# Wider products for the low-rank columns and the values of a hybrid decoder layer, and a shorter split of its norm weight

## The chip, the cores and the metric

The kernel runs on one core of a Trainium2 chip. The metric is the device time of one execution in microseconds: 638.64 us in the median of three runs before the change, between 638.29 and 639.48. Beside the times there is a profile of one execution, taken by the hardware profiler.

## The reference

One decoder layer with two parallel branches over 512 tokens of width 1024, everything in float32. `@` is a matrix product.

```python
h = rms_norm(x, norm_g)
hq, hf, hi, hz, cq, ckv, kr, mz, glog = split(h @ w_in)   # 4 x 1024 | 384 | 256 | 64 | 1024 | 2048
# branch a: 8 heads of 128, gated linear recurrence in chunks of 32 tokens
f = lb + (1 - lb) * sigmoid(hf);  q = silu(hq);  k = 1 - f;  v = hi
S_t = diag(f_t) S_{t-1} + k_t v_t^T;   o_t = S_t^T q_t
y_a = rms_norm(o per head, hg_norm_g) * silu(hz)
# branch b: 8 heads of attention over low-rank keys, queries and values
q    = rms_norm(cq, q_a_g) @ w_uq       # per head 128 without and 64 with a rotary position
k, v = rms_norm(ckv, kv_a_g) @ w_ukv    # per head 128 + 128; one rotary key kr for all heads
y_b  = softmax(causal(q k^T * scale)) v * silu(mz)
m = sigmoid(g_a) * (y_a @ w_proj_a) + sigmoid(g_b) * (y_b @ w_proj_b)   # g = glog + b_gate
out = rms_norm(x + m @ w_out, final_norm_g)
```

## The kernel before

Every large matrix product is done three times. An operand is split into a rounded high part and the rest (`hi`, `lo`), and `mm3` (L87) adds hi x hi, hi x lo and lo x hi in PSUM: its three matmuls are L90, L91 and L92. `load_w` (L94) brings a piece of weights of up to 128x1024 by SyncE's queue into one of three raw buffers, ScalarE rounds it (L111), VectorE subtracts (L112); there are four buffers each for the high and the low parts. Three PSUM tiles of 128x512 (`mm_tile`) take the large products, five more (`ax_tile`) the small ones.

The work runs in this order:

1. The start (L195 to L328), whose order on TensorE, ScalarE and VectorE is written out by hand. The norm weight comes as one row on one partition (L196), is split there (L270, L271), laid on the first row of two cleared tiles of 128x1024, and spread over all partitions by four matmuls with a matrix of ones (L274). Idle matmuls (`idle_mm`) stand between. Each 128-token tile of x is scaled by its norm factor and the spread weight (L237, `scaled`), turned by transposes (L245), and split into `hT` (L247, L248). The first 256 low-rank columns are multiplied in between (`c_product`, L256), and two weight loads for the next 256 are issued at the last tile (L320).
2. The other low-rank columns (L364): 256 and then 192, by `proj_tok` (L133). There a 128x128 block of `hT` is the stationary operand and the weights move, so one product is as wide as the columns. Two token tiles share a PSUM tile. The columns are normed and turned into `cT` (L368 to L396).
3. The recurrence, two heads at a time (`hg_pair`, L531). A pair has four stages of large products: forget, values, query and gate. Forget, query and gate are made by `proj_ch` (L120): the weights are stationary, `hT` moves with 512 tokens, and a stage fills two PSUM tiles. The values are made by `proj_tok` with 256 columns, two heads, and copied out by ScalarE (L538). From the forget product, VectorE and GpSimd make the decayed keys (`hg_forget`, L423: tanh L427, scan L432, reciprocal L433, then L448 to L451), from the query product `hg_query` makes the decayed queries (L459 to L463). Some working tiles there have one buffer for both heads.  `hg_states`, `hg_scores` and `hg_out` do the small products.
4. The attention, one head at a time (L691 to L711): scores and softmax, the rotary queries on every second head, the gate, the next head's keys and queries, the values of two heads on every even head (`mla_values`, L588: two k-steps, 256 columns), the product with the values of the head before (`mla_out`, L657) and the transposes of the probabilities (L652).
5. The merge of the branches (L730 to L743), the output product (L768 to L783) and the last norm, a token tile at a time. ScalarE scales and sends the first 512 columns of a tile (L793, L794), VectorE and SyncE's queue the others (L795, L796).

Behind the start, a scheduler puts the instructions of all engines in order when the program is built, by the order of the program and the times it estimates; an instruction that isn't ready can be passed by a later one then, but not when the program runs.

Of the kernel before, what the change touches and what calls it, by code (L numbers as in the profile page):

```python
# [9 lines left out]
F32 = mybir.dt.float32  # L10
# [28 lines left out]
def hybrid_layer(ctx: ExitStack, tc: tile.TileContext, a):  # L39
# [93 lines left out]
    def proj_tok(mat, c0, w, lhs, halves=None):  # L133

        halves = halves or load_cols(mat, c0, w)
        ps = []
        for t2 in range(NT // 2):
            b = mm_tile()
            for t in range(2):
                tt = 2 * t2 + t  # L140
                for kk in range(KD):
                    mm3(b[:, t * 256 : t * 256 + w], lhs, halves[kk // 4],
                        (slice(None), kk, slice(tt * P, tt * P + P)), (slice(None), kk % 4),
                        kk == 0, kk == KD - 1)
            ps.append(b)
        return ps
# [26 lines left out]
    ones = st.tile([P, P], F32, "ones")  # L173
    ones_r = st.tile([P, P], F32R, "ones_r")
    warm = st.tile([P, 1], F32, "warm")
    ng_row = st.tile([1, D], F32, "ng_row")
    ng_z = st.tile([P, D], F32, "ng_z")
    ng_r = [st.tile([P, D], F32R, f"ng_r{i}") for i in range(2)]
# [17 lines left out]
    nc.scalar.dma_start(ng_row[:], a["norm_g"])  # L196
# [61 lines left out]

    FIN = 1
    with tc.manual_schedule(engines={mybir.EngineType.PE, mybir.EngineType.Activation, mybir.EngineType.DVE}):  # L260
        nc.vector.memset(zero[:], 0.0)
# [8 lines left out]
        nc.vector.tensor_copy(ng_r[0][0:1], ng_row[:])  # L270
        nc.vector.tensor_tensor(ng_r[1][0:1], ng_row[:], ng_r[0][0:1].bitcast(F32), op=ALU.subtract)  # L271
        for x in range(2):
            for n in range(2):
                nc.tensor.matmul(ng[n][:], ones_r[:], ng_r[x][:, half[n]], start=x == 0, stop=x == 1)  # L274
            idle_mm(3)
# [36 lines left out]
        for t in range(1, NT):  # L312
# [153 lines left out]
    def hg_states(h, k128, ft, v_sb):  # L466
# [7 lines left out]
        for i in range(NT - 1):  # L474
            sl = slice(i * P, i * P + P)
            nc.tensor.matmul(sps[:, sl], kt_[:, sl], v_sb[:, i, (h % 2) * P : (h % 2) * P + P], start=True, stop=True)  # L476
# [25 lines left out]
    def hg_out(h, asb, st_, q128, v_sb):  # L502

        ops = ax_tile()
        for i in range(NT):
            sl = slice(i * P, i * P + P)
            nc.tensor.matmul(ops[:, sl], asb[:, sl], v_sb[:, i, (h % 2) * P : (h % 2) * P + P], start=True, stop=i == 0)  # L507
# [22 lines left out]

    def hg_pair(pair, before_gate=None, before_out=None):  # L531
# [159 lines left out]
    for h in range(H):  # L691
# [9 lines left out]
        if h % 2 == 0:  # L701
            v = mla_values(h // 2)
# [137 lines left out]
```

## Time and profile before

| | |
|---|---|
| median of three runs | 638.64 us |
| the profiled execution's own time | 638.65 us |
| its span, from the first to the last instruction | 636.9 us |
| TensorE busy | 627.3 us, 3539 matmuls |
| VectorE, ScalarE, GpSimd busy | 353.9, 239.4, 115.4 us |
| mean granted TensorE clock | 0.997 |
| moved by the DMA engines | 59.80 MB |

The profile is a page and a set of views on the trace of one execution. Engines are PE (TensorE matmul), PEld (TensorE weight load, which overlaps PE), DVE (VectorE), ACT (ScalarE), POOL (GpSimd) and SP (SyncE); a name with a q is that engine's queue of DMAs. A row of the timeline has the start in us, the duration in us, engine, line, operation, the tile written and those read, shapes, and how many instructions of one kind follow each other; behind it, in brackets, the idle time of the engine before it and what ended it. A group of the page has a count, the total busy time, the mean of one in ns, and the idle time in front. Matmuls are pipelined, so that their durations overlap: how long a stage takes is seen from starts.

### The profile page before, as it was taken

How to read it: one execution, taken by the hardware profiler on the slowest of the kernel's cores; microseconds unless marked ns; L12 is line 12 of the kernel's file. 1: busy time of each engine (PE TensorE's matmuls, PEld its weight loads, DVE VectorE, ACT ScalarE, POOL GpSimd, SP SyncE). 2: the span in 40 equal slices, each digit the busy share in tenths (PEclk: the TensorE clock that was granted, in tenths of full speed). 3: DMA queues.
4: the chain of work that ended last, by engine and by line, in shares of the span. 5: the costliest groups of instructions: out<-in, count | busy, mean ns of one | idle time of the engine just before them, and what ended most of it. 6: DMA issues, size and time to landing. Idle time of an engine off the chain costs nothing.

```text
span 636.9 us, 9069 instructions
## 1 busy us (share of the span) xinstructions
PE 627.3 (99%) x3539; PEld 540.1 (85%) x3539; DVE 353.9 (56%) x550; ACT 239.4 (38%) x453; POOL 115.4 (18%) x213
## 2 busy tenths in 40 slices
PE   8999999999999999999999999999999999999995
PEld 5998988988898898888888988888888888888884
DVE  7716973785486387547485857845322342434244
ACT  5535333232322323345454555534222232323223
POOL 2105310320331132221223132000000010111011
PEclk9999999999999999999999999999999999999998
DMA  7443242233124013312324142133333323324403
GB/s 248 137 125 100 67 138 62 67 99 100 34 68 131 13 55 102 92 45 66 104 56 115 51 138 78 37 100 99 100 98 94 98 75 102 102 95 158 173 11 121
DMA packets 61945, 59.80 MB, mean 94 GB/s; under 512 B 5799, under 2 KB 57293, under 8 KB 61902
## 3 DMA queue, kind: packets, MB, share of 16 engines
q1 hardware_dynamic: 59628, 55.47, 29.3%
q10 hardware_dynamic: 2130, 3.22, 1.6%
q8 instruction: 28, 0.46, 0.3%
q0 software_dynamic: 144, 0.52, 0.3%
q14 instruction: 15, 0.12, 0.1%
HBM read 55.01 MB, written 2.10 MB: 90 GB/s over the span
## 4 chain that ended last, share of the span: by engine, by line
PE 97%; DVE 1%; ACT 0%; issue 0%; POOLq 0%; POOL 0%
PE mm_ps L90 26%; PE mm_ps L92 26%; PE mm_ps L91 26%; PE ax_ps L91 2%; PE ax_ps L90 2%; PE ax_ps L92 2%; PE ax_ps L631 2%; PE mm_ps L256 1%; PE ax_ps L652 1%; PE ax_ps L488 1%; PE ax_ps L507 1%; PE ax_ps L509 1%; PE ax_ps L476 1%; PE ax_ps L496 1%; PE ax_ps L493 1%; PE ax_ps L523 1%
## 5 line engine op out<-in xcount | busy, mean ns | idle before, releaser
L112 DVE TENSOR_TENSOR w_lo<-w_raw,w_hi 128x1024 fp32r<-128x1024 f32 (+3 forms) x92 | 109.0, 1186 | 114.5 <-ACT w_hi L111 110.0
L90 PE MATMUL mm_ps<-hT,w_hi 128*128 128x512 f32 x384 | 151.3, 394 | 0.0
L111 ACT CAST w_hi<-w_raw 128x1024 fp32r<-128x1024 f32 (+3 forms) x92 | 89.8, 977 | 163.0 <-PE mm_ps L91 110.6
L92 PE MATMUL mm_ps<-hT,w_lo 128*128 128x512 f32 x384 | 150.2, 392 | 0.0
L91 PE MATMUL mm_ps<-hT,w_hi 128*128 128x512 f32 x384 | 149.8, 390 | 0.0
L92 PEld LDWEIGHTS mm_ps<-hT,w_lo 128*128 128x128 f32 x384 | 72.1, 188 | 14.8
L91 PEld LDWEIGHTS mm_ps<-hT,w_hi 128*128 128x128 f32 x384 | 72.2, 188 | 14.3
L90 PEld LDWEIGHTS mm_ps<-hT,w_hi 128*128 128x128 f32 x384 | 72.2, 188 | 14.1
L92 PE MATMUL mm_ps<-w_hi,hT 128*128 128x256 f32 (+1 forms) x192 | 54.1, 282 | 0.0
L91 PE MATMUL mm_ps<-w_lo,hT 128*128 128x256 f32 (+1 forms) x192 | 54.0, 282 | 0.0
L90 PE MATMUL mm_ps<-w_hi,hT 128*128 128x256 f32 (+1 forms) x192 | 54.0, 282 | 0.0
L742 POOL TENSOR_TENSOR ma<-ma,z 128x512 f32<-128x512 f32 x8 | 11.8, 1478 | 161.3 <-DVE z L741 161.3
L639 POOL TENSOR_SCALAR p<-p,sm 128x128 f32<-128x128 f32 (+3 forms) x32 | 20.6, 647 | 105.1 <-DVE sm L638 53.5
L91 PEld LDWEIGHTS mm_ps<-w_lo,hT 128*128 128x128 f32 x192 | 36.5, 190 | 0.2
L90 PEld LDWEIGHTS mm_ps<-w_hi,hT 128*128 128x128 f32 x192 | 36.4, 190 | 0.2
L92 PEld LDWEIGHTS mm_ps<-w_hi,hT 128*128 128x128 f32 x192 | 36.5, 190 | 0.0
L433 DVE RECIPROCAL tf<-pr 128x512 f32<-128x512 f32 x8 | 26.8, 3349 | 0.2
L637 ACT ACTIVATE p<-ax_ps,sm 128x128 f32<-128x128 f32 (+3 forms) x32 | 16.8, 528 | 22.0 <-DVE sm L636 21.5
L90 PE MATMUL mm_ps<-ya,w_hi 128*128 128x512 f32 x64 | 25.0, 390 | 0.0
L91 PE MATMUL mm_ps<-ya,w_hi 128*128 128x512 f32 x64 | 24.9, 389 | 0.0
L92 PE MATMUL mm_ps<-ya,w_lo 128*128 128x512 f32 x64 | 24.9, 389 | 0.0
L92 PE MATMUL mm_ps<-yb,w_lo 128*128 128x512 f32 x64 | 24.9, 389 | 0.0
(224 smaller groups left out, 1142.7 us busy)
## 6 DMA issues: line engine op xcount, KB each, us to landing
w_raw<-w_in SPq DMA_DIRECT2D x60, 512.0 KB, 3.8
w_raw<-w_proj_a SPq DMA_DIRECT2D x8, 512.0 KB, 3.5
w_raw<-w_proj_b SPq DMA_DIRECT2D x8, 512.0 KB, 3.4
wo_raw<-w_out SPq DMA_DIRECT2D x8, 512.0 KB, 3.2
w_raw<-w_ukv SPq DMA_DIRECT2D x16, 128.0 KB, 2.5
xr<-x SPq DMA_DIRECT2D x4, 512.0 KB, 6.5
x<-x SPq DMA_DIRECT2D x3, 512.0 KB, 8.7
w_raw<-w_uq SPq DMA_DIRECT2D x8, 192.0 KB, 2.6
```

Source lines behind the costliest of these rows:

```text
L90: nc.tensor.matmul(ps, lh[lsl], rh[rsl], start=start, stop=False)
L91: nc.tensor.matmul(ps, lh[lsl], rl[rsl], start=False, stop=False)
L92: nc.tensor.matmul(ps, ll[lsl], rh[rsl], start=False, stop=stop)
L111: nc.scalar.copy(hi[:, :o], raw[:, :o])
L112: (lo_eng or nc.vector).tensor_tensor(lo[:, :o], raw[:, :o], hi[:, :o].bitcast(F32), op=ALU.subtract)
L256: nc.tensor.matmul(ps, hT[l][:, 4 * kh + k, t * P : t * P + P], c_hl[kh][r][:, k * 256 : k * 256 + 256], start=kh == 0 and kind == 0 and k ...
L433: nc.vector.reciprocal(rp[:], pr[:])
L476: nc.tensor.matmul(sps[:, sl], kt_[:, sl], v_sb[:, i, (h % 2) * P : (h % 2) * P + P], start=True, stop=True)
L631: nc.tensor.matmul(sps[:, :n], qh[:, bl], kpe[x][:, :n], start=False, stop=x == 1)
L637: nc.scalar.activation(p[:, :n], sps[:, :n], AF.Exp, scale=SCALE, bias=sm[:, 1:2], accum_out=sm[:, 2:3])
L639: nc.gpsimd.tensor_scalar(p[:, :n], p[:, :n], sm[:, 3:4], 0.5, op0=ALU.mult, op1=ALU.mult)
L742: nc.gpsimd.tensor_tensor(ma[:, j], ma[:, j], g[:], op=ALU.add)
```

## The change

Five things are edited.

- The norm weight is laid as two rows of 512, on partitions 0 and 32 of a tile of 64 partitions, by two loads into a tile that GpSimd has cleared. It is split 512 wide. A selecting matrix (`pick`) takes the place of the ones, the clearing and copying of the large tiles on VectorE goes, and fewer idle matmuls stand between the first and the second pair of products (1 in place of 3; 4 in place of 3 behind the second).
- The low-rank columns are 256 and 448, not 256, 256 and 192. The weights come in four loads of two k-steps x 448; two are issued at the last tile of the start, two behind it. Each token tile has a PSUM tile of its own.
- The values of the recurrence are made for four heads at once, on pairs 0 and 2 alone: 512 columns, weights in four loads of two k-steps x 512. Two token tiles are done at a time, k outside and the tiles inside, so that the first two token tiles use all four loads and the second two use them again. They are kept in four tiles of 128x512 with one buffer each.
- The values of the attention are made for four heads at once, at heads 0 and 4, one token tile per PSUM tile, and kept in one buffer. They now stand behind the product with the head before.
- In the last norm the two halves of a tile lie in one buffer, and ScalarE and VectorE share the last token tile as 384 and 640 columns.

```diff
-    def proj_tok(mat, c0, w, lhs, halves=None):
-        halves = halves or load_cols(mat, c0, w)
-        ps = []
+    def proj_tok(mat, c0, lhs, done):
+        v = mat[:, c0 : c0 + 512].rearrange("(k p) c -> p k c", p=P)
+        w = []
         for t2 in range(NT // 2):
-            b = mm_tile()
+            ps = [mm_tile() for _ in range(2)]
+            for k in range(KD):
+                if t2 == 0 and k % 2 == 0:
+                    w.append(load_w(v[:, k : k + 2, :]))
+                for t in range(2):
+                    tt = 2 * t2 + t
+                    mm3(ps[t][:], lhs, w[k // 2], (slice(None), k, slice(tt * P, tt * P + P)), (slice(None), k % 2),
+                        k == 0, k == KD - 1)
             for t in range(2):
-                tt = 2 * t2 + t
-                for kk in range(KD):
-                    mm3(b[:, t * 256 : t * 256 + w], lhs, halves[kk // 4],
-                        (slice(None), kk, slice(tt * P, tt * P + P)), (slice(None), kk % 4),
-                        kk == 0, kk == KD - 1)
-            ps.append(b)
-        return ps
+                done(2 * t2 + t, ps[t])
...
+    ng_row = st.tile([64, 512], F32, "ng_row")
+    ng_r = [st.tile([64, 512], F32R, f"ng_r{i}") for i in range(2)]
+    nc.gpsimd.memset(ng_row[:], 0.0)
+    nc.gpsimd.memset(pick[:], 0.0)
+    for n in range(2):
+        nc.gpsimd.memset(pick[32 * n : 32 * n + 1, n], 1.0)
...
-    nc.scalar.dma_start(ng_row[:], a["norm_g"])
+    for n in range(2):
+        nc.scalar.dma_start(ng_row[32 * n : 32 * n + 1, :], a["norm_g"][:, n * 512 : n * 512 + 512])
...
+    w_c1 = w_in[:, COL_C + 256 : COL_C + 704].rearrange("(k p) c -> p k c", p=P)
+    def load_c2(j):
+        return load_w(w_c1[:, 2 * j : 2 * j + 2, :])
...
-        nc.vector.memset(ones[:], 1.0)
-        nc.vector.tensor_copy(ones_r[:], ones[:])
-        nc.vector.memset(ng_z[:], 0.0)
-        for i in range(2):
-            nc.vector.tensor_copy(ng_r[i][:], ng_z[:])
+        nc.vector.tensor_copy(pick_r[:], pick[:])
...
-        nc.vector.tensor_copy(ng_r[0][0:1], ng_row[:])
-        nc.vector.tensor_tensor(ng_r[1][0:1], ng_row[:], ng_r[0][0:1].bitcast(F32), op=ALU.subtract)
+        nc.vector.tensor_copy(ng_r[0][:], ng_row[:])
+        nc.vector.tensor_tensor(ng_r[1][:], ng_row[:], ng_r[0][:].bitcast(F32), op=ALU.subtract)
         for x in range(2):
             for n in range(2):
-                nc.tensor.matmul(ng[n][:], ones_r[:], ng_r[x][:, half[n]], start=x == 0, stop=x == 1)
-            idle_mm(3)
+                nc.tensor.matmul(ng[n][:], pick_r[:, n], ng_r[x][:], start=x == 0, stop=x == 1)
+            idle_mm(1 + 3 * x)
...
-                c_second = load_cols(w_in, COL_C + 256)
+                c_second = [load_c2(j) for j in range(2)]
...
-    for c0, w in ((0, 256), (256, 256), (512, 192)):
-        for t2, ps in enumerate(proj_tok(w_in, COL_C + c0, w, hT, c_second if c0 == 256 else None) if c0 else c_ps):
-            nc.scalar.copy(c_sb[:, 2 * t2 : 2 * t2 + 2, c0 : c0 + w],
-                           ps[:].rearrange("p (t c) -> p t c", t=2)[:, :, :w])
+    for t2, ps in enumerate(c_ps):
+        nc.scalar.copy(c_sb[:, 2 * t2 : 2 * t2 + 2, 0:256], ps[:].rearrange("p (t c) -> p t c", t=2))
+    c_second += [load_c2(j) for j in range(2, 4)]
+    for t in range(NT):
+        ps = mm_tile()
+        for k in range(KD):
+            mm3(ps[:, 0:448], hT, c_second[k // 2], (slice(None), k, slice(t * P, t * P + P)), (slice(None), k % 2),
+                k == 0, k == KD - 1)
+        nc.scalar.copy(c_sb[:, t, 256:704], ps[:, 0:448])
...
-        vps = proj_tok(w_in, COL_I + cc, 256, hT)
-        v_sb = hw.tile([P, NT, 256], F32, "v", 2)
-        for t2 in range(2):
-            nc.scalar.copy(v_sb[:, 2 * t2 : 2 * t2 + 2].rearrange("p t c -> p (t c)"), vps[t2][:])
+        if pair % 2 == 0:
+            for t in range(NT):
+                v_sb[t] = hw.tile([P, 512], F32, f"v{t}")
+            proj_tok(w_in, COL_I + cc, hT, lambda t, ps: nc.scalar.copy(v_sb[t][:], ps[:]))
...
-    def mla_values(pair):
-        wv = load_w(w_ukv[:, :, 2 * pair : 2 * pair + 2, 128:256])
-        v = [mw.tile([P, NT, 256], F32R, f"v{i}", 2) for i in range(2)]
-        for t2 in range(2):
+    def mla_values(h0):
+        wv = load_w(w_ukv[:, :, h0 : h0 + 4, 128:256])
+        v = [mw.tile([P, NT, 512], F32R, f"v{i}") for i in range(2)]
+        for t in range(NT):
             ps = mm_tile()
-            for t in range(2):
-                tt = 2 * t2 + t
-                for k in range(2):
-                    mm3(ps[:, t * 256 : t * 256 + 256], cT, wv, (slice(None), 3 + k, slice(tt * P, tt * P + P)),
-                        (slice(None), k), k == 0, k == 1)
-            split(*[x[:, 2 * t2 : 2 * t2 + 2].rearrange("p t c -> p (t c)") for x in v], ps[:])
+            for k in range(2):
+                mm3(ps[:], cT, wv, (slice(None), 3 + k, slice(t * P, t * P + P)), (slice(None), k), k == 0, k == 1)
+            split(v[0][:, t], v[1][:, t], ps[:])
...
-        if h % 2 == 0:
-            v = mla_values(h // 2)
         if late:
             mla_out(*late)
+        if h % 4 == 0:
+            v = mla_values(h)
...
-        nc.scalar.activation(rg[0][:], rg[0][:], AF.Copy, scale=ss[:, 0:1])
-        nc.scalar.dma_start(o[:, 0:512], rg[0][:])
-        nc.vector.tensor_scalar(rg[1][:], rg[1][:], ss[:, 0:1], None, op0=ALU.mult)
-        nc.sync.dma_start(o[:, 512:1024], rg[1][:])
+        c = 384 if last else 512
+        nc.scalar.activation(rg[:, :c], rg[:, :c], AF.Copy, scale=ss[:, 0:1])
+        nc.scalar.dma_start(o[:, :c], rg[:, :c])
+        nc.vector.tensor_scalar(rg[:, c:], rg[:, c:], ss[:, 0:1], None, op0=ALU.mult)
+        nc.sync.dma_start(o[:, c:], rg[:, c:])
```

More of the change, by code (lines that the diff above doesn't have):

```diff
@@ L172, in hybrid_layer @@
     zero = st.tile([P, 512], BF16, "zero")
-    ones = st.tile([P, P], F32, "ones")
-    ones_r = st.tile([P, P], F32R, "ones_r")
+    pick = st.tile([64, 2, P], F32, "pick")
+    pick_r = st.tile([64, 2, P], F32R, "pick_r")
     warm = st.tile([P, 1], F32, "warm")
-    ng_row = st.tile([1, D], F32, "ng_row")
-    ng_z = st.tile([P, D], F32, "ng_z")
-    ng_r = [st.tile([P, D], F32R, f"ng_r{i}") for i in range(2)]
+    ng_row = st.tile([64, 512], F32, "ng_row")
[4 more added lines that the diff above has]
+        nc.gpsimd.memset(pick[32 * n : 32 * n + 1, n], 1.0)
     x_sb = [st.tile([P, D], F32, "x", bufs=NT) for _ in range(NT)]
@@ L770, in hybrid_layer @@
         for t in range(NT):
-            for n in range(2):
-                out_mm(k, t, n, w)
+            for o in (0, 512):
+                out_mm(k, t, o, 512, w)
     ws = [load_wo(k) for k in range(4, KD)]
@@ L777, in hybrid_layer @@
     for t in range(NT):
[L778 to L781 removed]
+        last = t == NT - 1
+        ss = op.tile([P, 3], F32, "ss", bufs=2)
+        rg = op.tile([P, D], F32, "rg", bufs=2)
+        for i, (o, n) in enumerate(((0, 512), (512, 512))):
+            sl = slice(o, o + n)
             for k in range(4, KD):
[L783 to L784 removed]
+                out_mm(k, t, o, n, ws[k - 4])
+            nc.vector.scalar_tensor_tensor(xr[t][:, sl], acc[t][o // 512][:, o % 512 : o % 512 + n], 0.5, xr[t][:, sl],
+                                           op0=ALU.mult, op1=ALU.add)
             sq = op.tile([P, 512], F32, "sq", bufs=2)
[L786 to L790 removed]
+            nc.scalar.activation(sq[:, :n], xr[t][:, sl], AF.Square, accum_out=ss[:, i : i + 1])
+            nc.vector.tensor_tensor(rg[:, sl], xr[t][:, sl], fg[:, sl], op=ALU.mult)
+            nc.gpsimd.tensor_scalar(ss[:, 0:1], ss[:, i : i + 1], 1.0 / D, ss[:, 0:1] if i else EPS, op0=ALU.mult, op1=ALU.add)
         nc.gpsimd.tensor_tensor(ss[:, 0:1], ss[:, 0:1], neg_half[:, 0:1], op=ALU.pow)
         o = a["out"][0, t * P : t * P + P, :]
[L793 to L796 removed]
+        c = 384 if last else 512
[3 more added lines that the diff above has]
+        nc.sync.dma_start(o[:, c:], rg[:, c:])
     wop.close()
```

24 lines of the change are left out of this document (7 added, 17 removed).

## The prediction

> **What bounds the kernel now.** I read the page first, for the engine that carries the span and the chain that ended last.
>
> ```profile
> PE 627.3 (99%) x3539; PEld 540.1 (85%) x3539; DVE 353.9 (56%) x550; ACT 239.4 (38%) x453; POOL 115.4 (18%) x213
> ...
> PE 97%; DVE 1%; ACT 0%; issue 0%; POOLq 0%; POOL 0%
> ```
>
> TensorE is busy all the time and 97% of the chain is its own. A busy TensorE can still hide waits, so the view of waits, for TensorE alone, came next; its columns are the total, the number and the longest wait in us.
>
> ```profile
> PE ax_ps L221 <- DVE zero L261: 1.2, 1, 1.2
> PE ax_ps L274 <- DVE ng_r L270: 0.7, 1, 0.7
> PE ax_ps L245 <- DVE xn L237: 0.4, 1, 0.4
> PE mm_ps L256 <- ACT hT L247: 0.2, 1, 0.2
> PE mm_ps L256 <- DVE w_lo L228: 0.2, 1, 0.2
> ```
>
> These are all of its waits: 2.7 us, and every line named belongs to the start. Behind it, products follow each other at their own spacing. So the time is the sum of spacings plus the start and the tail, and the spacing is read from start to start in the timeline, not from the durations, which overlap.
>
> ```profile
> 117.97 0.28 PE L90 MATMUL mm_ps<-w_hi,hT 128*128 128x256 f32 x1
> ...
> 129.48 0.40 PE L90 MATMUL mm_ps<-hT,w_hi 128*128 128x512 f32 x1
> ...
> 140.43 0.27 PE L471 MATMUL ax_ps<-ident,k 128*128 128x128 f32 x1
> ```
>
> These are the first product of a value stage, the first of the query stage after it, and what follows that. The value stage has 4 tiles x 8 k x 3 = 96 products of 256 columns: 11.51 us, 0.120 each. The query stage has 2 x 8 x 3 = 48 of 512: 10.95 us, 0.228 each. Two products of 256 cost 0.240, one of 512 costs 0.228: 0.012 us per pair merged. The two prices make a line of 0.42 ns a column and some 12 ns fixed.
>
> **The change part by part.** *Low-rank columns, 256 + 192 become 448.*
>
> ```profile
> 27.30 0.39 PE L90 MATMUL mm_ps<-w_hi,hT 128*128 128x256 f32 x1
> ...
> 38.91 0.25 PE L90 MATMUL mm_ps<-w_hi,hT 128*128 128x192 f32 x1
> ...
> 49.61 0.41 PE L90 MATMUL mm_ps<-hT,w_hi 128*128 128x512 f32 x1
> ```
>
> 96 products of 256 take 11.61 us and 96 of 192 take 10.70 (0.111 each): 22.31 in all. A product of 448 isn't in this trace. Above it stands 512 with 0.228; below it 384, whose row is this:
>
> ```profile
> 308.95 0.33 PE L90 MATMUL mm_ps<-pt,v 128*128 128x384 f32 x1
> ...
> 309.48 0.28 PE L90 MATMUL mm_ps<-pt,v 128*128 128x256 f32 x1
> ```
>
> Three of 384 in 0.53 us are 0.177 each. Halfway between 0.177 and 0.228 lies 0.202, and the line gives 0.201. 96 x 0.201 = 19.3 us: 3.0 saved. The bounds are 0.4 (priced as 512) and 5.3 (as 384); I take 3.0, since both neighbours lie on one line.
>
> *Values of the recurrence, 4 x 96 of 256 become 2 x 96 of 512.* 4 x 11.51 = 46.0 us become 192 x 0.228 = 43.8: 2.3 saved. Nothing else of these stages changes in number: both make eight weight loads in two pairs and copy four full PSUM tiles.
>
> *Values of the attention, 96 of 256 become 48 of 512.* The old ones stand in short blocks between transposes:
>
> ```profile
> 357.39 0.49 PE L652 MATMUL ax_ps<-ident,p 128*128 128x128 f32 x3
> 357.64 0.37 PE L90 MATMUL mm_ps<-w_hi,cT 128*128 128x256 f32 x1
> ...
> 359.15 0.49 PE L652 MATMUL ax_ps<-ident,p 128*128 128x128 f32 x3
> ```
>
> Twelve take 1.51 us, so 96 take 11.5 to 12.1 (by 0.120 or by this block); 48 x 0.228 = 10.9: 0.7 saved.
>
> The Trainium skill speaks against this whole gain. Its page "TensorE: Matmul & The Clock Gate", section "Back-to-back issue gap", puts the spacing at columns / 2.4 + 2.5 ns. By it two halves cost only 2.5 ns more than the whole, and the 336 pairs merged here (96 + 192 + 48) would save an estimated 0.8 us. The rows above do not agree with its fixed part (some 12 ns here, not 2.5); this goes into the second rival.
>
> *Start.* These rows are from the first 13 us.
>
> ```profile
> 0.73 0.54 ACTq L196 DMA_DIRECT2D ng_row<-norm_g  x1
> ...
> 3.84 0.68 DVE L270 CAST ng_r<-ng_row 1x1024 fp32r<-1x1024 f32 x1
> 4.55 1.21 DVE L271 TENSOR_TENSOR ng_r<-ng_row,ng_r 1x1024 fp32r<-1x1024 f32 x1
> 6.54 1.41 PE L274 MATMUL ax_ps<-ng_r,ones_r 128*128 128x512 f32 x2
> 6.76 0.21 DVE L287 TENSOR_SCALAR rs<-rsq,rsq 128x1 f32<-128x1 f32 x1
> 7.56 1.41 DVE L237 SCALAR_TENSOR_TENSOR xn<-x,rs,ax_ps 128x512 f32<-128x512 f32 x2 [0.59 <-PE ax_ps L274]
> ...
> 8.88 0.76 DVE L224 CAST w_hi<-w_raw 128x512 fp32r<-128x512 f32 x2
> 12.08 0.67 DVE L228 TENSOR_TENSOR w_lo<-w_raw,w_hi 128x512 fp32r<-128x512 f32 x1
> ```
>
> The first scaling waits 0.59 us for the broadcast of the norm weight, though its other input is there at 6.97. After the change the cast and the subtraction are 512 wide: 0.38 and 0.67 in place of 0.68 and 1.21, and the clearing of the big tiles ahead of them is gone. Against it, the two loads of the row now wait for POOL to clear it, and there are two. ACT issues them, and what stands behind them on ACT is the table load and the squares of the first tile. From POOL's clearing of 128x512 and the spread of landing times (of x):
>
> ```profile
> 18.11 0.52 POOL L406 MEMSET fr<- 128x512 f32 x1
> ...
> DMA to landing us min/median/max: 2.7/3.8/8.7
> ```
>
> POOL's clearing of 64x512 has two short clearings ahead of it and ends near 1.4; the issues start at 1.4 and 1.95, and with 2.7 from the second the row is there near 4.65. The cast ends at 5.0, the subtraction at 5.7, the second pair of products (0.70 each) at 7.1, where its row ends at 7.95 now: 0.85 earlier, so the scale at 6.97 becomes the later input. ACT's first squares start about 1 us later than now, being queued behind the two issues, and the second half of x holds them until its landing in any case; I take the scale to come 0.2 later, so the scaling starts near 7.25: 0.3 gained. Ends: 0.55 gained (only the 6.97 left), and 0.3 lost (the row lands 3.8 after its issue, and the second pair ends at 8.25). Behind it the chain runs over DVE and TensorE up to the last wait of the list, so it is passed on.
>
> *Tail.* The last tile's scaling is cut 384/640 in place of 512/512.
>
> ```profile
> 632.58 0.72 ACT L793 ACTIVATE rg<-rg,ss 128x512 f32<-128x512 f32 x1 [1.10 <-POOL ss L791]
> 632.58 0.49 DVE L795 TENSOR_SCALAR rg<-rg,ss 128x512 f32<-128x512 f32 x1 [1.13 <-POOL ss L791]
> 633.09 0.33 SPq L796 DMA_DIRECT2D out<-rg  x1
> 633.33 0.34 ACTq L794 DMA_DIRECT2D out<-rg  x1
> ```
>
> ACT's part shrinks by at most a quarter of 0.72, DVE's grows by at most a quarter of 0.49, and they meet near 633.2: 0.1 gained. The rest of the norm at the end is written otherwise but issues the same instructions.
>
> *What comes late in return.* First, the second low-rank weights. Their four loads are all used within the first token tile, the last of them after 18 products, at 27.3 + 18 x 0.201 = 30.9; before, it was used from 38.91 on. It waits for a raw buffer, and today the fourth load is there as follows:
>
> ```profile
> 29.98 0.82 ACT L111 CAST w_hi<-w_raw 128x768 fp32r<-128x768 f32 x1
> ...
> 30.82 0.96 DVE L112 TENSOR_TENSOR w_lo<-w_raw,w_hi 128x768 fp32r<-128x768 f32 x1 [0.56 <-ACT w_hi L111]
> ```
>
> With 896 columns these are 0.96 and 1.12, so the low half is there at 32.0, 0.9 after its first use. TensorE can run the next tile's first products in that time if the scheduler foresees it: 0 to 0.9, I take 0.4.
>
> Second, the odd pairs of heads. They lose the value stage that stood between the forget and the query products. These rows are of pair 1; the second fence is the windows view over one pair (busy us of PE, PEld, DVE, ACT and POOL in turn); the third is the page's row of the weight splits.
>
> ```profile
> 123.67 0.60 ACT L427 ACTIVATE tf<-mm_ps 128x512 f32<-128x512 f32 x1 [4.68 <-DVE ki L448]
> 126.91 1.23 DVE L432 TENSOR_TENSOR_SCAN pr<-f,fr 128x512 f32<-128x512 f32 x1 [1.47 <-POOL fr L429]
> 128.17 3.35 DVE L433 RECIPROCAL tf<-pr 128x512 f32<-128x512 f32 x1
> ...
> 138.54 0.69 DVE L459 SCALAR_TENSOR_TENSOR f<-f,mm_ps 128x512 f32<-128x512 f32 x1 [1.24 <-ACT f L458]
> ```
>
> ```profile
> 157.80:212.60 54.80, 54.80 (x359) 48.37 (x359) 34.71 (x40) 16.55 (x34) 11.78 (x30) 1.00 0.27 74
> ```
>
> ```profile
> L112 DVE TENSOR_TENSOR w_lo<-w_raw,w_hi 128x1024 fp32r<-128x1024 f32 (+3 forms) x92 | 109.0, 1186 | 114.5 <-ACT w_hi L111 110.0
> ```
>
> Put the query stage at 117.97: it ends at 128.9, and the gate stage's second PSUM tile is wanted 12 products later, at 131.7. Only three such tiles exist; this one still holds the first query head until L459 has read it. DVE reaches L459 after the reciprocal (131.5) and three more steps of the second head like L459's own (0.69 each): L459 ends at 134.3, 2.6 late. TensorE has other work then (the gate's second half into its first tile, 12 x 0.228 = 2.7 us), and blocks like that of 357.64 show the order of the program being left where something waits. DVE has 34.71 of 54.80 us now; an odd pair would have 32.3 of 43.3 (two splits of 1.19 and 11.5 us of TensorE less), so it doesn't become the bound on average. Price 0 to 2.6 for each of two such pairs; I take 0.3 each.
>
> In an even pair the first value pass takes two tiles at once and four weights in 10.9 us. The tile that DVE holds longest, by L427 until 124.3, is wanted for the second pass at 128.9: nothing.
>
> Third, attention heads 2 and 6 lose the value products that filled gaps between transposes; heads 0 and 4 get more. The two blocks of such a head are 3.0 us; waits there lie between 0 and that, and the next head's gate can fill them: 0.2 in all.
>
> **Sum.** -3.0 - 2.3 - 0.7 - 0.3 - 0.1 + 0.4 + 0.6 + 0.2 = -5.2 us, from the profiled execution's 638.65 (its span of 636.9 and 1.75 around it); the median of the runs is 638.64, the same. That gives 633.4.
>
> **Rivals.** *One: the query tile holds TensorE in the odd pairs.* If the products stay in the order written, each odd pair waits 2.6 us, and with two weight splits of 1.19 ahead of L459, 5.0. For it: DVE is the second engine, and its reciprocal alone is 3.35. Against: no wait at all after the start today. It gives 638.65 - 5.2 - 0.6 + 5.2 = 638.0, or 642.8 with the splits (10.0 in place of 5.2): slower by over 0.2% from some 3.5 us an odd pair on, (5.8 + 1.3) / 2. Chances 0.08 for the first, 0.07 for the second.
>
> *Two: width buys nothing, the cost goes by columns.* If a wide product cost what its halves cost (0.240 for 512, 0.231 for 448), the 6.0 us vanish and 639.4 is left. Against it stands 0.228 over 48 products in the same kernel. Chance 0.02. With the page's 2.5 ns a pair it would be an estimated 638.6.
>
> *Three: the four weights of a value pass come late.* Each wants a cast on ACT and a split of 1.19 on DVE, and two must wait for buffers of the forget stage; the fourth is wanted 36 products or 8.2 us into the pass. For it: DVE's reciprocals stand in that stretch. Against: it needs a queue of some 6 us. Price one split, 1.2, for each of two passes: 635.8. Chance 0.07, counted as faster.
>
> **How the numbers follow.** The forecast, with its own spread of the unknowns, has 0.76: from 632.0 (none of the 1.2 us of costs and a start at 0.55) to 636.0 (448 priced as 512). With the third rival, faster by over 0.2% (1.3 us, about what a measurement of this kernel can tell) has 0.83; within it 0.10 (first rival's mild form, second); slower 0.07. The range of 631.6 to 637.6 begins a little below the first of these, for the lower bound of 448, and takes in the third rival and what lies between the forecast and the first.
>
> **What would show it.** Spacings of 0.228 for the 512 value products and 0.20 for 448; the stage from the first low-rank product to the first forget product at 19 to 20 us; the first scaling near 7.25; no TensorE wait after 30 us beyond a few tenths. A wait on DVE L459 or on w_lo in the view of waits, of some us in total, would make it wrong; so would 448 priced like 512.

## The result: slower by 5.5 us, and the profile after

The changed kernel takes 644.49 us in the median of four runs (644.02 to 645.43), the kernel before 638.97 on the same chip (four runs, 638.29 to 639.48): a ratio of 1.0089, with a 95% interval of 1.0071 to 1.0106. The forecast was 633.4. The profiled execution took 644.26 us, with a span of 642.5.

First the page of the kernel after, engines and chain:

```profile
PE 625.7 (97%) x3202; PEld 525.5 (82%) x3202; DVE 349.8 (54%) x544; ACT 239.1 (37%) x451; POOL 121.5 (19%) x217
...
PE 93%; DVE 2%; issue 1%; POOL 1%; DMA 1%; ACT 0%; POOLq 0%; ACTq 0%; DVEq 0%
```

TensorE has 337 matmuls fewer, but its share of the chain fell from 97% to 93%: there are waits now. TensorE's view of waits names them (total, number, longest, in us):

```profile
PE mm_ps L90 <- DVE f L472: 3.9, 2, 2.9
PE ax_ps L282 <- DVE ng_r L278: 2.8, 1, 2.8
PE mm_ps L90 <- ACT pt L151: 1.2, 1, 1.2
PE ax_ps L227 <- DVE zero L273: 1.2, 1, 1.2
```

The last of the four was there before, and the second was 0.7 us (L274). The first three belong to one edited stage each: the query products' reader in the recurrence, the split of the norm weight, and the last transposed probabilities of the attention. The timeline shows each. The start:

```profile
0.73 0.40 ACTq L203 DMA_DIRECT2D ident<-c_ident  x1
0.79 0.52 POOL L180 MEMSET ng_row<- 64x512 f32 x1
1.34 0.76 ACTq L202 DMA_DIRECT2D ng_row<-norm_g  x2
6.24 0.42 DVE L278 CAST ng_r<-ng_row 64x512 fp32r<-64x512 f32 x1 [3.88 <-DMA ng_row<-norm_g]
6.71 0.73 PE L282 MATMUL ax_ps<-ng_r,pick_r 64*128 64x512 f32 x2 [2.79 <-DVE ng_r L278]
8.74 1.41 DVE L243 SCALAR_TENSOR_TENSOR xn<-x,rs,ax_ps 128x512 f32<-128x512 f32 x2 [0.16 <-PE ax_ps L282]
9.06 1.89 PE L227 MATMUL ax_ps<-zero 128*128 128x512 bf16 x4
10.74 1.91 PE L251 MATMUL ax_ps<-ident,xn 128*128 128x128 f32 x8
...
30.20 0.47 PE L90 MATMUL mm_ps<-w_hi,hT 128*128 128x448 f32 x1
49.77 0.39 PE L90 MATMUL mm_ps<-hT,w_hi 128*128 128x512 f32 x1
```

The row's loads are issued at 1.34 instead of 0.73, behind the clearing and now behind the load of the identity, and the cast starts at 6.24 instead of 3.84. The first scaling is 1.18 us late (8.74 for 7.56), the first of the wide low-rank products 2.90 (30.20 for 27.30). The other 1.7 us arise at the transposes (L251), whose row before was this:

```profile
8.67 1.04 PE L245 MATMUL ax_ps<-ident,xn 128*128 128x128 f32 x8
```

They start 2.07 late, for the four idle products at 9.06 stand ahead of them, and the eight then take 0.8 longer, from start to start. From the first wide low-rank product to the first forget product it is 19.57 us instead of 22.31, so that the forget products begin only 0.16 later than before.

The first product behind the scores of the last pair of heads stands 4.3 us later than before (277.18 for 272.86). What lies between, in the timeline from pair 3: VectorE and ScalarE first, then TensorE.

```profile
251.87 0.63 DVE L472 SCALAR_TENSOR_TENSOR f<-f,mm_ps 128x512 f32<-128x512 f32 x1
252.42 1.21 DVE L112 TENSOR_TENSOR w_lo<-w_raw,w_hi 128x1024 fp32r<-128x1024 f32 x1
254.35 0.68 DVE L474 TENSOR_TENSOR qi<-f,pr 128x512 f32<-128x512 f32 x1
254.95 1.22 DVE L112 TENSOR_TENSOR w_lo<-w_raw,w_hi 128x1024 fp32r<-128x1024 f32 x1
256.08 1.11 DVE L462 TENSOR_TENSOR ko<-ki,pr 128x512 f32<-128x512 f32 x1
257.38 1.13 DVE L476 TENSOR_TENSOR q<-qi,gh 128x512 f32<-128x512 f32 x1
258.43 0.68 DVE L472 SCALAR_TENSOR_TENSOR f<-f,mm_ps 128x512 f32<-128x512 f32 x1
...
255.06 0.60 ACT L471 ACTIVATE f<-mm_ps 128x512 f32<-128x512 f32 x1 [3.06 <-DVE qi L474]
```

```profile
252.56 0.50 PE L90 MATMUL mm_ps<-cT,w_hi 128*128 128x512 f32 x1 [0.99 <-DVE f L472]
...
259.16 0.50 PE L90 MATMUL mm_ps<-hT,w_hi 128*128 128x512 f32 x1 [2.91 <-DVE f L472]
259.98 0.63 PE L90 MATMUL mm_ps<-hT,w_hi 128*128 128x512 f32 x1
260.41 0.63 PE L91 MATMUL mm_ps<-hT,w_hi 128*128 128x512 f32 x1
```

L472 (L459 before) reads a query head out of its PSUM tile. For the first head it runs at 251.87, for the second at 258.43: ScalarE may write `f` again only when L474 has read it (3.06 us of waiting), and VectorE has two weight splits and three steps in between. Before, the two stood at 248.19 and 252.32, and nobody waited. What wants the tile is in the rows of TensorE: in the last pair, products of `cT` (rotary queries, queries and keys of the first attention head) take three more tiles ahead of the gate.

The rows at 259.98 show a second loss: products of 512 are 0.43 us apart there, not 0.228. In TensorE's windows view (length, busy, count, granted clock, DMA share, GB/s) one stretch has it, of before and then of after:

```profile
259.20:263.40 4.20, 4.20 (x23) 1.00 0.45 125
```

```profile
259.20:263.40 4.20, 4.20 (x12) 0.59 0.00 0
```

From 259.98 to 263.37 there are eight products that would have taken 1.8 us: 1.6 lost to the half clock behind the wait.

At the end of the attention TensorE waits once more. The first product with `ya` stood at 421.40 before; in the timeline after it stands at 426.90:

```profile
424.39 0.93 PE L664 MATMUL ax_ps<-ident,p 128*128 128x128 f32 x7
426.57 0.50 PE L90 MATMUL mm_ps<-pt,v 128*128 128x512 f32 x1 [1.25 <-ACT pt L151]
426.90 0.39 PE L90 MATMUL mm_ps<-ya,w_hi 128*128 128x512 f32 x1
```

Behind that nothing changes: 5.50 us late here, 5.6 at the end of the span.

So from the first wide low-rank product to the first product with `ya` the stretch grew from 394.1 to 396.7 us. Added up from start to start, without the waits, the products of `hT` and `cT` with moving weights take 5.6 us less (74.7 for 80.3), near the 6.0 forecast for the width. The waits of the stretch, 5.3 us, and the half clock's 1.6 gave that back with 1.3 more; the 1.3 us left over are spread over the other products, and no run shows their cause.

### The profile page after: what moved, and what is told of

Read it like the earlier page. It is cut to its first block, busy times and chain, and to the rows that moved or that the text cites. A ratio compares the mean times of both kernels' runs of the same rounds, so it can differ in the third digit from the quotient of the medians.

```text
span 642.5 us, 8395 instructions
## 1 busy us (share of the span) xinstructions
PE 625.7 (97%) x3202; PEld 525.5 (82%) x3202; DVE 349.8 (54%) x544; ACT 239.1 (37%) x451; POOL 121.5 (19%) x217
## 4 chain that ended last, share of the span: by engine, by line
PE 93%; DVE 2%; issue 1%; POOL 1%; DMA 1%; ACT 0%; POOLq 0%; ACTq 0%; DVEq 0%
PE mm_ps L90 25%; PE mm_ps L91 25%; PE mm_ps L92 25%; PE ax_ps L90 2%; PE ax_ps L92 2%; PE ax_ps L91 2%; PE mm_ps L262 2%; PE ax_ps L643 2%; PE ax_ps L664 1%; PE ax_ps L501 1%; PE ax_ps L520 1%; PE ax_ps L522 1%; PE ax_ps L509 1%; PE ax_ps L489 1%; PE ax_ps L251 1%
## 5 line engine op out<-in xcount | busy, mean ns | idle before, releaser
L92 PE MATMUL mm_ps<-w_hi,hT 128*128 128x512 f32 (+1 forms) x96 | 36.7, 384 | 0.0
L91 PE MATMUL mm_ps<-w_lo,hT 128*128 128x512 f32 (+1 forms) x96 | 36.5, 382 | 0.0
L90 PE MATMUL mm_ps<-w_hi,hT 128*128 128x512 f32 (+1 forms) x96 | 36.0, 384 | 0.0
L90 PE MATMUL mm_ps<-yb,w_hi 128*128 128x512 f32 x64 | 24.9, 390 | 0.0
L91 PE MATMUL mm_ps<-yb,w_hi 128*128 128x512 f32 x64 | 24.9, 389 | 0.0
L152 DVE TENSOR_TENSOR wo<-wo_raw,wo 128x1024 fp32r<-128x1024 f32 x8 | 9.6, 1225 | 25.9 <-ACT wo L151 25.9
```

What stands on the lines that cost most here:

```text
L90: nc.tensor.matmul(ps, lh[lsl], rh[rsl], start=start, stop=False)
L91: nc.tensor.matmul(ps, lh[lsl], rl[rsl], start=False, stop=False)
L92: nc.tensor.matmul(ps, ll[lsl], rh[rsl], start=False, stop=stop)
L152: nc.vector.tensor_tensor(lo, src, hi.bitcast(F32), op=ALU.subtract)
```

## The experiments

The theory behind the first runs: the merged products save what was forecast, and each of three edits (start, recurrence values, attention values) brings a wait that costs more than its saving. The rival: one cause in common, such as a start whose delay disturbs what follows. Every run is compared with the kernel before on the same chip.

**The start alone** (the new split of the norm weight; the rest as before).

> The kernel before with the new split of the norm weight alone (two rows, two loads behind GpSimd's clearing, selecting matrix). Theory: the start alone costs what the changed kernel shows there, its first low-rank product at 30.2 us instead of 27.3, because the second row lands near 6 us; about 641.8 us. Rival: the late landing comes of what the other edits move in the order of the queues; then this one is within 0.5 us of before, 638.5 to 639.4.

641.48 us for 638.97, ratio 1.0042 (1.0027 to 1.0057). The timeline:

```profile
5.96 0.42 DVE L271 CAST ng_r<-ng_row 64x512 fp32r<-64x512 f32 x1 [3.61 <-DMA ng_row<-norm_g]
...
8.96 0.75 DVE L242 SCALAR_TENSOR_TENSOR xn<-x,rs,ax_ps 128x512 f32<-128x512 f32 x1 [0.64 <-PE ax_ps L275]
```

The first product of the second low-rank columns stands at 30.15, as in the kernel after (30.20), and the 394.1 us behind it are those of before. The start costs 2.5 us by itself.

**The low-rank columns alone** (256 + 448).

> The kernel before with the low-rank columns as 256 + 448 alone. Theory: 96 products at 0.202 us replace 96 at 0.120 and 96 at 0.111, 2.7 us saved as in the changed kernel, with no new wait; about 636.2. Rival: the saved time is lost again to a wait farther on, in the recurrence; about 639.

636.21 us, ratio 0.9958 (0.9941 to 0.9974): 2.8 saved. From the first wide low-rank product at 27.80 to the first forget product at 47.37 it is 19.57 us, as in the kernel after (0.204 each), and no wait is new. The second weights that were to come 0.4 late cost nothing.

**The recurrence values alone** (four heads on pairs 0 and 2).

> The kernel before with the recurrence's values for four heads alone. Theory: 2.3 us saved in the products, and TensorE waits some 4 us for the query step L459 of the last pair and then runs at the half clock for 3.4 us, 1.8 us lost: about 642. Rival: the waits of the last pair come only with the shifted start and low-rank stage; then about 636.7.

641.31 us, ratio 1.0041 (1.0026 to 1.0056). TensorE's view of waits:

```profile
PE mm_ps L90 <- DVE f L475: 3.9, 2, 2.9
```

It is the wait of the kernel after, to a tenth, without the new start: so no common cause. In this profile the clock stays at 1.00 behind the wait, which was not expected; the half clock does not follow every time.

**The attention values alone** (four heads at heads 0 and 4).

> The kernel before with the attention's values for four heads alone. Theory: 0.6 us saved in the products, and the wait of 1.4 us ahead of the last head's product with the values, seen in the changed kernel, belongs to this edit: about 639.7. Rival: that wait comes of other edits; about 638.3.

640.61 us, ratio 1.0032 (1.0019 to 1.0045), 0.9 more than expected. TensorE's waits behind the start:

```profile
PE mm_ps L90 <- ACT pt L150: 1.2, 1, 1.2
PE mm_ps L90 <- DVE qn L151: 0.4, 1, 0.4
PE ax_ps L649 <- POOL p L636: 0.4, 2, 0.2
```

Beside the wait at the end there are small ones at 344 to 346 us, which the kernel after doesn't have. How the end differs is seen in TensorE's timeline, of before and of this kernel:

```profile
416.92 0.49 PE L652 MATMUL ax_ps<-ident,p 128*128 128x128 f32 x3
417.16 0.49 PE L90 MATMUL mm_ps<-hT,w_hi 128*128 128x512 f32 x1
...
420.03 0.60 PE L652 MATMUL ax_ps<-ident,p 128*128 128x128 f32 x4
420.39 0.48 PE L90 MATMUL mm_ps<-hT,w_hi 128*128 128x512 f32 x1
```

```profile
421.16 0.39 PE L92 MATMUL mm_ps<-hT,w_lo 128*128 128x512 f32 x1
421.39 0.93 PE L649 MATMUL ax_ps<-ident,p 128*128 128x128 f32 x7
423.57 0.50 PE L90 MATMUL mm_ps<-pt,v 128*128 128x512 f32 x1 [1.25 <-ACT pt L150]
```

Before, the last transposes stood in two groups among gate products, which covered the copies out of PSUM. Head 6 has no value products now, so that the gate products are spent earlier; the seven transposes come last, in one group, and their copies are waited for. That this is the reason is read from the order of the rows; the run with 2, 4 and 2 heads below tests it.

**The last norm alone** (384 and 640 columns at the last tile).

> The kernel before with the last norm as in the change alone (one buffer for a tile's halves, the last tile cut as 384 and 640). Theory: 0 to 0.1 us, not to be told from before, 638.5 to 639.0. Rival: the one buffer makes one engine's write wait for the other's; then the end of TensorE to the end of the span grows from 6.9 to over 7.5.

638.75 us for 638.70, ratio 1.0001 (0.9991 to 1.0011): nothing.

**What holds TensorE in the last pair.** Three versions of the kernel with the recurrence values alone. In the first, the large products have four PSUM tiles and the small ones four, and the idle products' tile is one of the large:

```diff
-N_MM = 3
+N_MM = 4
-    idle = ax_tile()
+    idle = mm_tile()
```

> Four-head recurrence values alone, with four PSUM tiles for the large products and four for the small ones, in place of three and five. Theory: TensorE waits in the last pair because a query's PSUM tile isn't read yet; with one more tile both waits on that step go or fall below 1.2 us in sum, and 636.7 to 638 is left, if the small products don't wait for their four. Rival: TensorE waits for the data that VectorE makes, not for a tile; then the sum of waits in the last pair stays near 4 us, about 641.

637.27 us for 638.78, ratio 0.9977 (0.9968 to 0.9987). The wait on `f` is gone, and one at the end of the attention has come:

```profile
PE mm_ps L90 <- ACT pt L166: 1.0, 1, 1.0
```

VectorE is hardly earlier here: the second head's query is read at 257.18 (257.85 without the fourth tile), but no product needs its tile: the gate's products start at 254.57, ahead of that read, and at 258.58 without the fourth tile. The tile is what held.

In the second version the wide stage stands on pair 1, for heads 2 to 5, and pairs 0 and 3 make two heads each:

```diff
-        if pair % 2 == 0:
+        if pair != 2:
             for t in range(NT):
                 v_sb[t] = hw.tile([P, 512], F32, f"v{t}")
+        if pair == 1:
             proj_tok4(w_in, COL_I + cc, hT, lambda t, ps: nc.scalar.copy(v_sb[t][:], ps[:]))
+        elif pair != 2:
+            for t2, ps in enumerate(proj_tok(w_in, COL_I + cc, 256, hT)):
+                for t in range(2):
+                    nc.scalar.copy(v_sb[2 * t2 + t][:, 0:256], ps[:, t * 256 : t * 256 + 256])
```

> Recurrence values made for heads 0-1, then 2-5 on pair 1, then 6-7, so that the last pair keeps a value stage and pair 2 goes without; nothing else changed from before. Theory: a pair without value stage waits only where the attention's first rope, query and key products want PSUM tiles too, and that is the last pair; so no TensorE wait over 0.3 us is left after the start, and half of the 2.3 us is saved: about 637.8. Rival: any pair without value stage is too short for VectorE; then pair 2 waits some 4 us: about 641.5.

637.35 us, ratio 0.9976 (0.9967 to 0.9986), and TensorE waits nowhere behind the start. Pair 2 does without a value stage and nothing waits; so it is not the missing stage as such, but the missing stage in the pair that also makes the first attention head.

In the third, the rotary, query and key products of the last pair move behind its gate products:

```diff
-        if before_gate:
-            before_gate()
         pz = proj_ch(w_in, COL_ZA + cc, hT)
...
+        if before_gate:
+            before_gate()
         aa = [hg_scores(h, kk[i][2], kk[i][3], kk[i][4], qq[i][0], qq[i][1]) for i, h in enumerate(hs)]
```

> Four-head recurrence values alone, with the attention's first rope, query and key products of the last pair put behind its gate product. Theory: the gate then finds the tile that the forget product left, as in pair 1, and by the time of rope the queries are read: waits in the last pair under 1 us in sum, about 637.3. Rival (VectorE is late with the last pair as a whole): the wait comes back ahead of the scores, some 3 to 4 us, about 641.

641.24 us, ratio 1.0036 (1.0023 to 1.0049). The wait moved; its row is now

```profile
PE ax_ps L539 <- DVE k L531: 2.9, 1, 2.9
```

and stands at 291.62 us. VectorE is behind with this pair as a whole, so this other order of TensorE only finds the next place to wait; more PSUM, or more work for TensorE, did away with the wait.

**The attention values as 2, 4 and 2 heads** (256 columns at heads 0 and 6, 512 at head 2; the core of the edit):

```diff
-        if h % 4 == 0:
+        if h in (0, 2, 6):
             v = mla_values(h)
```

> Attention values for heads 0-1, then 2-5, then 6-7; the rest as before. Theory: the four-head form lost 2.5 us because heads 6 and 7 have no value products left to stand between scores and transposes, so that the gate of the last head is used up early and nothing covers the rounding of the last probabilities; with head 6 having its own, the 1.4 us wait at the end goes, and with 0.3 us saved it is 638.4 to 638.9. Rival: the wait comes of the order in which the values now stand behind the product with the head before; then it stays, about 640.5.

639.34 us for 638.78, ratio 1.0005 (0.9995 to 1.0014). With value products in heads 2 and 6 again the wait at the end is gone, and most of the 1.6 us with it; but 24 merges save nothing that can be measured.

**What makes the start late.** Three versions of the kernel with the start alone. First, the identity comes by SyncE's queue, behind the first tile of x and the first weights:

```diff
-    nc.scalar.dma_start(ident[:], a["c_ident"])
     load_c(0)
+    nc.sync.dma_start(ident[:], a["c_ident"])
```

> The new split of the norm weight alone, with the identity matrix loaded from SyncE's queue behind x and the first weights, so that ScalarE's queue carries nothing but the two rows. Theory: the rows are late because the wait for GpSimd's clearing lets the identity's load go ahead of them; now the cast L270's successor starts by 4.3 instead of 6.0 us: about 639.0. Rival: the second row is late because it starts after x and the first weights have filled the DMA engines, whatever stands ahead of it on its own queue: the cast stays near 6 us, about 641.5.

640.11 us for 638.64, ratio 1.0019 (1.0007 to 1.0032). Its timeline:

```profile
4.66 0.42 DVE L271 CAST ng_r<-ng_row 64x512 fp32r<-64x512 f32 x1 [2.31 <-DMA ng_row<-norm_g]
5.14 1.22 PE L275 MATMUL ax_ps<-ng_r,pick_r 64*128 64x512 f32 x2 [1.22 <-DVE ng_r L271]
```

The loads of the row are issued at 1.34, as in the run of the start alone, and the cast starts 1.3 earlier: the identity's load ahead of them was that much of the delay. That is less than expected (by 4.3), and so is the gain. The first scaling starts at 7.66, only 0.1 later than in the kernel before, and the first product of the second low-rank columns still stands 1.5 later, at 28.84: the four idle products behind the second pair run until 9.66, and the transposes behind them are 0.21 us apart, as in the kernel after, instead of 0.11. The ten runs lie between 637.95 and 641.44, so the start's cost varies from one execution to the next.

Second, each half of the row is loaded into 32 partitions at once, and nothing is cleared first:

```diff
-    nc.gpsimd.memset(ng_row[:], 0.0)
...
-        nc.scalar.dma_start(ng_row[32 * n : 32 * n + 1, :], a["norm_g"][:, n * 512 : n * 512 + 512])
+        nc.scalar.dma_start(ng_row[32 * n : 32 * n + 32, :], a["norm_g"][0, n * 512 : n * 512 + 512].partition_broadcast(32))
```

> The new split alone, without GpSimd's clearing: each half of the row is loaded into 32 partitions, so that the two loads wait for nothing and stand first in ScalarE's queue; 128 KB are moved in place of 4. Theory: the wait for the clearing is what makes the rows late; the cast starts by 3.6 us and the first scaling near 7.1: about 638.5. Rival (two loads, not the wait): the cast stays near 6 us, about 641.5.

639.58 us, ratio 1.0017 (1.0008 to 1.0026). The cast stands at 4.72, 1.1 later than expected although the issues are back at 0.73: these two loads, of 64 KB each as they are spread, land later than the one load of the row did. The scaling starts at 7.72 and the first product of the second low-rank columns at 28.25.

Third, on top of that, TensorE is kept busier: nine idle products ahead of the first pair of products, then one and two.

```diff
-        idle_mm(6)
+        idle_mm(9)
...
-            idle_mm(1 + 3 * x)
+            idle_mm(1 + x)
```

> As the run that loads each half into 32 partitions, but with 9 idle matmuls ahead of the first norm product in place of 6, 1 between and 2 behind in place of 1 and 4. Theory: the new start loses most of its time by the clock, because TensorE rests 1.2 us or more before the first norm product, and the full clock comes at 10 to 13 us in place of 8 to 10; with the rest filled the first low-rank product starts by 27.8: about 638.5. Rival: the late first scaling alone sets it, and idle matmuls change nothing: 28.2, about 639.5.

638.54 us for 638.70, ratio 1.0004 (0.9994 to 1.0013). Its timeline:

```profile
4.94 0.42 DVE L270 CAST ng_r<-ng_row 64x512 fp32r<-64x512 f32 x1 [3.04 <-DMA ng_row<-norm_g]
5.41 0.73 PE L274 MATMUL ax_ps<-ng_r,pick_r 64*128 64x512 f32 x2 [0.32 <-DVE ng_r L270]
7.39 1.41 DVE L241 SCALAR_TENSOR_TENSOR xn<-x,rs,ax_ps 128x512 f32<-128x512 f32 x2
```

The cast comes 0.2 later than without the extra idle products, and yet everything behind it earlier: two products take 0.73 us instead of 1.22, the scaling starts at 7.39, the first product of the second low-rank columns at 27.73. By the medians (639.58 and 638.54, each beside before on its chip) the edit brings back about 1 us, all that this start still cost. What does it is not separated: it changes the idle products ahead of the first pair and also leaves two where four stood ahead of the transposes, which start at 8.20 instead of 9.72. The clock by itself doesn't explain it. In this profile the granted clock is 1.00 up to 8 us and then 0.50 from 9 to 11, the eight transposes take 1.94 us (1.22 without the extra idle products), and the low-rank products still come earlier.

**Together.** First the change with the start of before:

> The changed kernel with the start of before. Theory: the parts measured one by one add: the low-rank columns 2.8 saved, the recurrence's values 2.3 lost, the attention's 1.6 lost: about 640.0, and the half clock behind the last pair's wait is seen in some executions only, with up to 1.9 more. Rival: the parts spoil each other besides the clock; then over 642.5.

640.31 us in seven runs (639.67 to 641.57), ratio 1.0028 (1.0017 to 1.0039). Its profiled execution took 641.04, with the wait on `f` of 3.9 us and the half clock behind it. Over before on its own chip it loses 1.6 us, where the kernel after loses 5.5; the profiled executions, both with the half clock, are 3.2 apart. By itself the new start cost 2.5. The 0.7 between 3.2 and 2.5 is no more than the start of before differs with itself: its first product of the second low-rank columns stands at 26.80 here, at 27.30 in the kernel before and at 28.13 in the run with attention values 2, 4, 2.

Then what paid, in one kernel: the low-rank columns as 256 and 448, the recurrence values of four heads with four PSUM tiles, the new last norm, and start and attention values as before.

> The start and the attention's values of before; low-rank columns as 256 + 448, four-head values in the recurrence, the tail cut as 384 and 640, and four PSUM tiles for the large products with four for the small. Theory: the parts add, 2.7 saved by the low-rank columns and 1.5 by the recurrence with the fourth tile, 0 to 0.1 by the tail: about 634.5. Rival: with fewer small tiles and less slack they don't add: 636 or more.

634.73 us for 638.64 (634.14 to 635.21), ratio 0.9940 (0.9925 to 0.9955): the fastest of all, ahead of both kernels by 3.9 and 9.8 us. The same with the recurrence values as 2, 4 and 2 heads and three tiles:

> The start and the attention's values of before; low-rank columns as 256 + 448, recurrence values for heads 0-1, 2-5 and 6-7, the tail cut as 384 and 640, three PSUM tiles as before. Theory: 2.7 and 1.4 saved add up: about 634.6. Rival: the shorter low-rank stage ahead of pair 0 and a pair 2 without value stage together bring back a wait on the query step: 636 or more.

635.00 us, ratio 0.9945 (0.9930 to 0.9960), and no wait of TensorE behind the start.

## Why the prediction was wrong, step by step

**The width: right.** The low-rank term was -3.0 and measured -2.8 alone, at 0.204 us a product of 448 where 0.201 was worked out. Over the stretch behind the start the merged products took 5.6 us less; the three terms for the width were 6.0.

**The second low-rank weights: +0.4 forecast, nothing measured.** No wait in the run of the low-rank columns alone.

**The start: the step that put the row's landing near 4.65 failed.** It let the row land 2.7 us, the shortest of the page's landings, behind the second issue. The cast began at 6.24. Two things were left out: that the identity's load, which waits for nothing, would pass ahead of the row's loads (1.3 us of it, by its own run), and what TensorE does meanwhile: a rest of 2.8 us, and four idle products ahead of the transposes. The bounds, 0.55 gained to 0.3 lost, held only the landing, and "it is passed on" took the delay of the scaling for the whole. The 1.2 us at the first scaling became 2.9 at the low-rank products: 0.9 more because the transposes wait for the idle products, which are 0.43 us apart, and 0.8 because they are themselves 0.21 apart and not 0.11. The granted clock goes with that: 0.50 from 8 to 14 us after, 1.00 before. How much of it is the edit's is open. With the start of before unchanged, products come to their full spacing near 5 us in the run with the start of before, at 8.3 in the kernel before and at 10.6 in the run with attention values 2, 4, 2, and the low-rank products follow in that order (26.80, 27.30, 28.13). The medians of the runs, not these single traces, show that the new start costs 2.5 us.

**The odd pairs: the step that priced both alike, 0.3 each, failed.** The mechanism was named, L459 and the query tile, and so was its range of 0 to 2.6; but the price was taken from pair 1, and "TensorE has other work then" was taken for both. Pair 1 costs nothing. In pair 3 three more tiles are wanted ahead of the gate, by the rotary, query and key products, and only three exist: 3.9 us in two waits, which the run with four PSUM tiles takes away. That is between the rival's 2.6 and 5.0, for one pair instead of two. The half clock behind it, 1.6 us where it comes, was in no term.

**The attention: the term of 0.2 was mis-sized.** The step said that the next head's gate can fill the gaps of heads 2 and 6. It can, but then it is missing where the probabilities of the last head are transposed, and there is no next head. Alone the edit cost 1.6 us; with 0.7 saved by width, the lost filling is worth 2.3.

**The tail: 0.1 forecast, nothing measured.** ScalarE and VectorE meet as worked out:

```profile
638.13 0.62 ACT L806 ACTIVATE rg<-rg,ss 128x384 f32<-128x384 f32 x1 [1.10 <-POOL ss L803]
638.14 0.55 DVE L808 TENSOR_SCALAR rg<-rg,ss 128x640 f32<-128x640 f32 x1 [1.13 <-POOL ss L803]
...
638.78 0.34 ACTq L807 DMA_DIRECT2D out<-rg  x1
```

The last issue comes 0.65 us behind the scaling's start instead of 0.75, but the span ends 3.70 behind it instead of 3.54.

**The sum.** By the runs alone, in the order in which they stand above: +2.51 - 2.76 + 2.34 + 1.64 + 0.05 = +3.8; measured, +5.5. The half clock's 1.6 in pair 3 would make it 5.4, if the run of the recurrence values alone was mostly without it, as its profiled execution was, and the four runs of the kernel after all with it; neither is shown. Against this reading, the same sum without the start is +1.3, and the run with the start of before lost 1.6, with the half clock in its profiled execution. So 1.4 of the missing 1.7 us come only together with the new start (5.5 less 1.6 less 2.5), and why stays open.

**Still open.** Why the half clock follows the same wait in some executions only. Whether a second buffer for `f` alone would free the query tile in time was not tried.

## What to carry to other kernels

Wider products gave what their spacing promised; what took it back was that narrow stages between two others are also time in which a second engine catches up. Before a stage is merged away, walk through each of its places, count the PSUM tiles wanted between the last product and the late reader in that place, and price the worst of them, above all the first and last round, where other work joins or runs out. Small loads at a start are worth an eye on what passes ahead of them, and on how many idle products then stand ahead of the first real ones.

## What the runs showed of the hardware

A wait of 2.9 us was followed by eight products of 512 at 0.43 us, for 3.4 us, in the kernel after, and by none in the run of the recurrence values alone. It came back in the run of the change with the start of before. At the start the rest alone doesn't tell the spacing: the first two products of the norm weight took 1.22 us behind a rest of 1.28, 0.73 behind one of 0.32 with three more idle products, but also 0.73 behind one of 2.79, in the kernel after. Nor does the granted clock always: in the run of the start alone it reads 1.00 from 10 to 14.2 us, though products are at twice their full spacing there until about 13.2. The Trainium skill, page "TensorE: Matmul & The Clock Gate", part 1, describes a window of some 3.4 us that runs freely, half clock after an idle one, and warm-up that differs from run to run. The 3.4 us agree with it, and so does the scatter. That a wait of 2.9 us, shorter than a window, can be enough is shown by the trace.

GpSimd's scaling of the last 128 x 512 probabilities took 0.69 us in the kernel before and 1.52 with the attention values alone; in the latter it shares the time with VectorE's work. The timelines of GpSimd, before and then with the attention values alone:

```profile
415.15 0.69 POOL L639 TENSOR_SCALAR p<-p,sm 128x512 f32<-128x512 f32 x1 [4.95 <-DVE sm L638]
```

```profile
419.87 1.52 POOL L636 TENSOR_SCALAR p<-p,sm 128x512 f32<-128x512 f32 x1 [1.98 <-DVE sm L635]
```

That the sharing is the cause is argued from the rows, not shown.
